# Seven block products for eight in the gate and up projections of a two-layer model

## The chip, the cores and the metric

One Trainium2 chip, one core of it. The metric is the device time of one execution in microseconds (us); the kernel before took 3628.52 us, the median of three runs (3627.12 to 3630.19). TensorE is called PE here, VectorE DVE, ScalarE ACT, GpSimd POOL, and SP is the engine that issues the DMAs.

## The reference, cut to what matters

A model of 512 tokens of width 1024 in float32: two layers of one kind, then two of another. Each of the latter is a feed-forward, a hybrid mixer and a second feed-forward, so the block below runs four times, with 1024 x 2816 gate and up weights and 2816 x 1024 down weights:

```python
def rmsnorm(x, w):
    xf = x.astype(jnp.float32)
    y = xf * lax.rsqrt(jnp.mean(xf * xf, axis=-1, keepdims=True) + EPS)
    return (y * w.astype(jnp.float32)).astype(x.dtype)

def swiglu(h, w_gate, w_up, w_down):
    return (jax.nn.silu(h @ w_gate) * (h @ w_up)) @ w_down
...
        x = x + 0.5 * swiglu(rmsnorm(x, norm_ffn1[layer]), ffn1_gate[layer], ffn1_up[layer],
                             ffn1_down[layer])
```

## The kernel before, in words

Activations lie feature-major: tile `X` is 128 partitions x 8 chunks x 512 tokens. Float32 products are made of three matmuls in a rounded format: every operand is split into a high part (ACT copies it into the rounded type) and a low part (DVE subtracts the high part from the original), and `mm3` adds high x high, high x low and low x high into one PSUM bank. So a product of a 1024-long contraction into 128 features is 8 x 3 matmuls, each with a 128x128 weight block loaded and 512 tokens streamed.

Weights come in one stream, `wall`: chunks of 128 x 512 floats, that is four 128x128 blocks, in the order in which they are used. `wfill` issues the DMA of a chunk on SP (256 KB), splits it on ACT and DVE, and runs `LOOK` = 3 chunks ahead; `w` hands out the blocks. High and low parts have four buffers each (`p_hi`, `p_lo`), raw chunks four.

`ffn` calls `rms_begin`, which splits X times the gain into `XH` and `XL` and makes `rb`, the reciprocal root of each token, on 128 partitions; since `rb` depends on the token alone it is multiplied into the products' results. Then J = 22 pairs follow: for each block of 128 hidden features a gate and an up product through `fm_seq` (the first three products interleaved over k, the others one by one). A gate result is multiplied by `rb` on DVE (L602) and goes through Silu on ACT (L603); an up result is multiplied by `rb` (L606) and by the gate (L607), and the pair is split at once into `HH` and `HL`, tiles of 22 chunks. The down products, m = 0 to 7, contract over the 22 chunks of `HH` and `HL`; each is added with weight 0.5 into `X[:, m]` (L612). In the very last feed-forward the eighth down product runs in two halves of 256 tokens.

The order of the instructions on an engine isn't that of the code: the framework sets it when the program is built, and an instruction can pass one that stands ahead of it in the code but isn't ready yet. Only what stands in `pin` keeps its place. A buffer of a pool is given to its next tile when the last use of the one before is over.

Of the kernel before, what the change touches and what calls it, by code (L numbers as in the profile page):

```python
# [7 lines left out]
F32 = mybir.dt.float32  # L8
F32R = mybir.dt.float32r
I32 = mybir.dt.int32  # L10
AF = mybir.ActivationFunctionType
OP = mybir.AluOpType
# [3 lines left out]
T = 512  # L16
D = 1024
KD = 8
DFF1 = 4096
DFF2 = 2816  # L20
CH = 512
NCH = 1104
NCOL = 332
NROW = 168
LOOK = 3
# [37 lines left out]
class Parts:  # L63


    def __init__(self, parts):
        self.parts = parts

    def __getitem__(self, i):
        return self.parts[i[1]]  # L70


class K:
    def __init__(self, tc, ap, inp):
        self.tc, self.nc, self.ap, self.inp = tc, tc.nc, ap, inp
        self.es = ExitStack()
        self.wall = np.zeros((NCH, 128, CH), np.float32)
        self.cols_a = np.zeros((128, NCOL), np.float32)
        self.rows_a = np.zeros((1, NROW), np.float32)
        self.ncol = 0  # L80
        self.nrow = 0
        self.wpos = 0
        self.wemit = 0
        self.look = LOOK
        self.wt = {}

    def pool(self, name, bufs, **k):
# [2 lines left out]

    def wfill(self, upto, pin=lambda i: i):
        nc = self.nc
        while self.wemit < min(upto, NCH):
            c = self.wemit
            raw = self.p_raw.tile([128, CH], F32, name="wraw")
            nc.sync.dma_start(out=raw, in_=self.ap['wall'][c])
            hi = self.p_hi.tile([128, CH], F32R, name="whi")
            pin(nc.scalar.activation(hi, raw, AF.Copy))  # L98
            lo = self.p_lo.tile([128, CH], F32R, name="wlo")
            pin(nc.vector.tensor_tensor(out=lo, in0=raw, in1=hi.bitcast(F32), op=OP.subtract))  # L100
            self.wt[c] = (hi, lo)
# [366 lines left out]
    def first_layer(self, i):  # L468
# [3 lines left out]
        with ExitStack() as es:  # L472
# [35 lines left out]
            for half in range(2):  # L508
                hh = []
                for name, n in HT[i]:  # L510
                    t = pool.tile([128, n, T], F32R, name=name)
                    hh += [t[:, k] for k in range(n)]
                HH, HL = Parts(hh[:16]), Parts(hh[16:32])
                o = half * 2048
                for m, ps in enumerate(self.fm_seq(XH, XL, [w1[:, o + m * 128:o + (m + 1) * 128] for m in range(16)])):
# [69 lines left out]


    def ffn(self, i, n):
        nc, inp = self.nc, self.inp
        with ExitStack() as es:
            pool = es.enter_context(self.tc.tile_pool(name="ffn%d%d" % (i, n), bufs=1, reuse_waits="tile"))  # L590
            XH, XL, y, rb = self.rms_begin(self.cols(inp['norm_ffn%d_2' % n][i]), pool if n == 2 else None)
            wg, wu, wd = [inp['ffn%d_%s_2' % (n, z)][i] for z in ('gate', 'up', 'down')]
            J = DFF2 // 128
            HH = pool.tile([128, J, T], F32R, name="HH")
            HL = pool.tile([128, J, T], F32R, name="HL")
            ws = []
            for j in range(J):
                ws += [wg[:, j * 128:(j + 1) * 128], wu[:, j * 128:(j + 1) * 128]]
            for j, ps in enumerate(self.fm_seq(XH, XL, ws)):
                if j % 2 == 0:  # L600
                    g1 = self.p_wk.tile([128, T], F32, name="t0")
                    nc.vector.tensor_tensor(out=g1, in0=ps, in1=rb, op=OP.mult)  # L602
                    nc.scalar.activation(g1, g1, AF.Silu)  # L603
                    continue
                u1 = self.p_wk.tile([128, T], F32, name="t1")
                nc.vector.tensor_tensor(out=u1, in0=ps, in1=rb, op=OP.mult)  # L606
                nc.vector.tensor_tensor(out=u1, in0=u1, in1=g1, op=OP.mult)  # L607
                self.split(HH[:, j // 2], HL[:, j // 2], u1)
            last = i == 1 and n == 2
            for m in range(7 if last else 8):  # L610
                ps = self.fm(HH, HL, wd[:, m * 128:(m + 1) * 128])
                nc.vector.scalar_tensor_tensor(out=self.X[:, m], in0=ps, scalar=0.5, in1=self.X[:, m], op0=OP.mult, op1=OP.add)  # L612
                if last:
                    self.sum_sq(m)
            if last:
                ws = [self.w(wd[k * 128:(k + 1) * 128, 896:]) for k in range(J)]
                self.out = self.p_x.tile([128, 8, T], F32, name="XH")
                for half in range(2):
                    s = slice(half * 256, half * 256 + 256)
                    ps = self.dps()  # L620
                    for k, (wh, wl) in enumerate(ws):
                        self.mm3(ps[:, :256], wh, wl, HH[:, k, s], HL[:, k, s], k == 0, k == J - 1)
                    self.final(half, s, ps[:, :256])
        return self.stop("ffn%d_%d" % (n, i))
# [1281 lines left out]
```

## Time and profile before

| | us |
|---|---|
| median of three runs | 3628.52 |
| the profiled execution's own time | 3626.38 |
| its span, first to last instruction | 3624.6 |
| PE busy | 3537.3 (98%) |
| DVE busy | 1980.6 (55%) |
| ACT busy | 1534.8 (42%) |
| POOL busy | 395.6 (11%) |

The shares are of the span and average over unlike stages. Matmuls overlap: a busy time of 389 ns for one says nothing of the step from one to the next, which is read from a timeline. The granted clock of PE was 0.995 of its full speed over the span.

### The profile page before, as it was taken

The page shows a single profiled execution, that of the slowest core. Times are in us where ns is not written, and L with a number is a line of the kernel's source. Part 1 is how long each engine was busy: PE and PEld are TensorE (multiplying, and loading weights), DVE is VectorE, ACT ScalarE, POOL GpSimd, SP SyncE. Part 2 cuts the span into 40 slices and gives each one's busy share as a digit, 9 for nine tenths or more (in the row PEclk, how much of TensorE's full clock was granted, in tenths as well). Part 3 has the DMA queues.
Part 4 walks back from the last instruction along what each step waited for, and adds up shares of the span by engine and source line. Part 5 has one row for each costly group of instructions (what it writes and reads, how often), then busy time and mean ns, then how long its engine had stood idle before and what let it go on. Part 6 is the DMA issues. An engine that isn't in the chain of part 4 may idle for free.

```text
span 3624.6 us, 46983 instructions
## 1 busy us (share of the span) xinstructions
PE 3537.3 (98%) x17270; PEld 2892.1 (80%) x17270; DVE 1980.6 (55%) x3841; ACT 1534.8 (42%) x2827; POOL 395.6 (11%) x402
## 2 busy tenths in 40 slices
PE   9999999999999999999999999999999999999999
PEld 7766888876678887888887888888888888888887
DVE  4686534467764346544368655543454378665443
ACT  4554524256643334433365533333333366443332
POOL 0003000203030003000012410000000012410000
PEclk9999999999999999999999999999999999999999
DMA  4112333332023332333332113333333332013332
GB/s 155 53 39 73 93 98 97 90 95 62 18 83 98 96 97 81 96 96 98 97 104 69 36 39 94 96 99 97 94 98 97 96 106 70 19 50 97 99 96 88
DMA packets 165976, 304.37 MB, mean 84 GB/s; under 512 B 19824, under 2 KB 20976, under 8 KB 165360
## 3 DMA queue, kind: packets, MB, share of 16 engines
q1 hardware_dynamic: 165744, 301.36, 28.6%
q8 instruction: 135, 2.21, 0.2%
q14 instruction: 97, 0.79, 0.1%
HBM read 299.19 MB, written 2.10 MB: 83 GB/s over the span
## 4 chain that ended last, share of the span: by engine, by line
PE 80%; DVE 6%; ACT 3%; issue 2%; POOL 1%; DVEq 0%; POOLq 0%; ACTq 0%
PE pd L246 24%; PE pd L245 24%; PE pd L247 24%; PE pt L264 1%; DVE wlo L100 1%; PE pd L1515 1%; PE ps L1503 1%; PE po L1747 0%; PE pd L1700 0%; ACT whi L98 0%; PE pd L1224 0%; DVE rep L1192 0%; PE ps L1239 0%; PE ps L1178 0%; PE ps L1240 0%
## 5 line engine op out<-in xcount | busy, mean ns | idle before, releaser
L100 DVE TENSOR_TENSOR wlo<-wraw,whi 128x512 fp32r<-128x512 f32 x1104 | 793.6, 720 | 1041.9 <-ACT whi L98 999.7
L98 ACT ACTIVATE whi<-wraw 128x512 fp32r<-128x512 f32 x1104 | 695.6, 631 | 1487.8 <-PE pd L246 1254.3
L245 PE MATMUL pd<-XH,whi 128*128 128x512 f32 x2752 | 1080.0, 394 | 22.2 <-DVE t L235 5.4
L246 PE MATMUL pd<-XL,whi 128*128 128x512 f32 x2752 | 1080.1, 392 | 12.1 <-DVE XL L411 9.5
L247 PE MATMUL pd<-XH,wlo 128*128 128x512 f32 x2752 | 1080.2, 393 | 0.0
L245 PEld LDWEIGHTS pd<-XH,whi 128*128 128x128 f32 x2752 | 518.6, 189 | 138.0 <-DVE t L235 6.3
L246 PEld LDWEIGHTS pd<-XL,whi 128*128 128x128 f32 x2752 | 520.0, 189 | 125.4 <-DVE XL L411 11.2
L247 PEld LDWEIGHTS pd<-XH,wlo 128*128 128x128 f32 x2752 | 519.6, 189 | 110.6 <-issue 2.6
L245 PE MATMUL pd<-HH,whi 128*128 128x512 f32 (+1 forms) x726 | 278.1, 383 | 0.0
L247 PE MATMUL pd<-HH,wlo 128*128 128x512 f32 (+1 forms) x726 | 277.7, 383 | 0.0
L246 PE MATMUL pd<-HL,whi 128*128 128x512 f32 (+1 forms) x726 | 277.6, 383 | 0.0
L454 POOL TENSOR_TENSOR acc<-acc,t 128x512 f32<-128x512 f32 x36 | 47.3, 1315 | 1162.3 <-ACT t L453 1151.4
L245 PEld LDWEIGHTS pd<-HH,whi 128*128 128x128 f32 x726 | 136.4, 188 | 26.9
L247 PEld LDWEIGHTS pd<-HH,wlo 128*128 128x128 f32 x726 | 136.4, 188 | 26.6
L246 PEld LDWEIGHTS pd<-HL,whi 128*128 128x128 f32 x726 | 136.4, 188 | 26.6
L606 DVE TENSOR_TENSOR t<-pd,rb 128x512 f32<-128x512 f32 x88 | 60.8, 691 | 86.7 <-PE pd L247 86.7
L602 DVE TENSOR_TENSOR t<-pd,rb 128x512 f32<-128x512 f32 x88 | 60.8, 691 | 82.7 <-PE pd L247 82.7
L245 PE MATMUL pd<-CQHL,whi 128*128 128x512 f32 x224 | 88.8, 397 | 0.0
L247 PE MATMUL pd<-CQHL,wlo 128*128 128x512 f32 x224 | 88.0, 393 | 0.0
L260 ACT ACTIVATE HH<-t 128x512 fp32r<-128x512 f32 x88 | 55.7, 633 | 50.6 <-DVE t L607 50.6
L344 POOL COPY acc<-X 128x512 f32<-128x512 f32 x4 | 3.1, 777 | 676.5 <-DVE X L342 527.9
L261 DVE TENSOR_TENSOR HL<-t,HH 128x512 fp32r<-128x512 f32 x88 | 60.9, 692 | 21.0 <-ACT HH L260 14.9
(809 smaller groups left out, 4945.0 us busy)
## 6 DMA issues: line engine op xcount, KB each, us to landing
wraw<-in_wall_dram SPq DMA_DIRECT2D x1104, 256.0 KB, 2.6
X<-in_xT_dram SPq DMA_DIRECT2D x8, 256.0 KB, 5.7
cw<-in_cw_dram SPq DMA_DIRECT2D x2, 1024.0 KB, 6.3
X<-in_xT_dram SPq DMA_DIRECT2D x1, 2048.0 KB, 8.2
out_dram<-XH SPq DMA_DIRECT2D x8, 256.0 KB, 2.7
t<-in_pT_dram SPq DMA_DIRECT2D x4, 256.0 KB, 2.8
LV<-in_cst_dram SPq DMA_DIRECT2D x2, 512.0 KB, 4.0
g_dT<-in_rgw_dram SPq DMA_DIRECT2D x2, 256.0 KB, 3.8
```

What stands on the lines that cost most here:

```text
L98: pin(nc.scalar.activation(hi, raw, AF.Copy))
L100: pin(nc.vector.tensor_tensor(out=lo, in0=raw, in1=hi.bitcast(F32), op=OP.subtract))
L245: t.matmul(ps, ah, bh, start=first, stop=False)
L246: t.matmul(ps, ah, bl, start=False, stop=False)
L247: t.matmul(ps, al, bh, start=False, stop=last)
L260: self.nc.scalar.activation(hi, src, AF.Copy)
L261: self.nc.vector.tensor_tensor(out=lo, in0=src, in1=hi.bitcast(F32), op=OP.subtract)
L264: self.nc.tensor.transpose(out, src, self.ID[:kp, :kp])
L454: (nc.vector if c == 7 else nc.gpsimd).tensor_tensor(out=acc, in0=acc, in1=sq, op=OP.add)
L602: nc.vector.tensor_tensor(out=g1, in0=ps, in1=rb, op=OP.mult)
L606: nc.vector.tensor_tensor(out=u1, in0=ps, in1=rb, op=OP.mult)
L1503: nc.tensor.matmul(pz[:, h], B[:, h], Xt[c][:, h], start=True, stop=True)
```

## The change: block products of Strassen's kind, and a result kept whole

Of the 22 pairs of a feed-forward the pairs 5 to 20 go through a new class, `Strassen`. It takes gate and up together as a matrix of two block rows (128 gate features, 128 up features) and two block columns (inputs 0 to 511 and 512 to 1023), and the tokens as two halves of 256. The 2 x 2 block product is then made from seven block products in the place of eight, with sums of weight blocks (s1 to s4, made on the chip for each pair) and sums of activation blocks (t0 to t3, made once a feed-forward), in Winograd's form: results of products are added up in PSUM over several of them, and partly on DVE and ACT.

- A `product` is 4 row blocks x 3 matmuls of 256 columns, 12 matmuls. `cycle(j)` issues seven: four of pair j into banks A, D and B with the weights a11, a12, s1 and s2, the fifth with s4, and between them two of pair j - 1 (s3 and a22) into its bank A.
- `load` fetches the four raw chunks of the next pair; `pa` splits a12 and a11, `sums` makes two sums, `ps` a third one and splits two of them; `ring` splits a block into the buffers of the weight stream.
- `c12` finishes the gate of the pair before, `c22` and `c21` the up part and the product into `H`.
- The activations must be normalised ahead, since sums of tokens' halves mix tokens with unlike `rb`: `prepare` makes X times gain times `rb` in `H[:, 14:22]`, the four sums and their splits `TH` and `TL`, during the five plain pairs. `renew` then overwrites `XH` and `XL` with the normalised ones.
- The pair's result stays in `H`, in whole float32, and is split into `HH` and `HL` only around the down products; these parts lie in the memory of tiles that are no longer needed. The first three down products run interleaved over k, the others one by one, and in the first feed-forward of a layer the last one begins with the low parts 16 to 21.
- The last pair, 21, is a plain one on the normalised activations, without `rb`.

```diff
...
@@ -67,7 +67,176 @@
         self.parts = parts
     def __getitem__(self, i):
-        return self.parts[i[1]]
+        p = self.parts[i[1]]
+        return p if len(i) == 2 else p[:, i[2]]
+class Strassen:
+    def __init__(self, k, pool, wg, wu, XH, XL, TH, TL, H):
+        self.k, self.nc, self.pool, self.wg, self.wu, self.H = k, k.nc, pool, wg, wu, H
+        self.XH, self.XL, self.TH, self.TL = XH, XL, TH, TL
+        self.R, self.u, self.prev = {}, {}, None
+        for name, n in self.PLACES:
+            pool.tile([128, n, T], F32, name=name)
+    PLACES = [("R0", 4), ("R1", 4), ("ST", 4), ("AH", 2), ("AL", 2), ("SH", 2), ("SL", 2), ("HX", 2)]
...
+    def prepare(self, X, gain, rb):
+        nc, H = self.nc, self.H
...
+        for c in range(8):
+            nc.vector.scalar_tensor_tensor(out=XN[:, c], in0=X[:, c], scalar=gain[:, c:c + 1], in1=rb, op0=OP.mult, op1=OP.mult)
+            if c % 2:
+                yield
+        b = lambda r, t: XN[:, 4 * r:4 * r + 4, 256 * t:256 * t + 256]
+        t = [H[:, 6 + 2 * q:8 + 2 * q].rearrange("p a (h t) -> p (a h) t", h=2) for q in range(4)]
+        nc.vector.tensor_tensor(out=t[0], in0=b(0, 0), in1=b(0, 1), op=OP.subtract)
+        yield
+        nc.vector.scalar_tensor_tensor(out=t[1], in0=t[0], scalar=-1.0, in1=b(1, 1), op0=OP.mult, op1=OP.subtract)
+        yield
+        nc.vector.tensor_tensor(out=t[2], in0=b(1, 1), in1=b(0, 1), op=OP.subtract)
+        yield
+        nc.vector.tensor_tensor(out=t[3], in0=b(0, 0), in1=b(1, 0), op=OP.subtract)
+        yield
+        nc.vector.tensor_tensor(out=t[3], in0=t[3], in1=t[2], op=OP.add)
+        yield
+        for q in range(4):
+            nc.scalar.activation(self.TH[:, q], t[q], AF.Copy)
+            yield
+            nc.vector.tensor_tensor(out=self.TL[:, q], in0=t[q], in1=self.TH[:, q].bitcast(F32), op=OP.subtract)
+            yield
+    def renew(self):
+        for c in range(8):
+            self.k.split(self.XH[:, c], self.XL[:, c], self.XN[:, c])
+    def load(self, j, c):
+        nc, k = self.nc, self.k
+        R = self.R[j] = self.pool.tile([128, 4, T], F32, name="R%d" % (j % 2))
+        s = slice(j * 128, (j + 1) * 128)
+        for q, (w, o) in enumerate(((self.wg, 4), (self.wg, 0), (self.wu, 4), (self.wu, 0))):
...
+        for q in (0, 1, 3, 2):
+            nc.sync.dma_start(out=R[:, q], in_=k.ap['wall'][c + q])
...
+    def ring(self, j, what, src):
+        hi, lo = self.k.p_hi.tile([128, CH], F32R, name="whi"), self.k.p_lo.tile([128, CH], F32R, name="wlo")
+        self.k.split(hi, lo, src)
+        self.u[j, what] = hi, lo
+    def pa(self, j):
+        hi, lo = self.parts("A", self.R[j][:, 0:2])
+        self.u[j, "a12"], self.u[j, "a11"] = [(hi[:, q], lo[:, q]) for q in range(2)]
+    def sums(self, j):
+        nc, R = self.nc, self.R[j]
+        S = self.S = self.pool.tile([128, 4, T], F32, name="ST")
+        nc.vector.tensor_tensor(out=S[:, 0:2], in0=R[:, 1:3], in1=R[:, 3:4].to_broadcast([128, 2, T]), op=OP.add)
+    def ps(self, j):
+        S = self.S
+        self.nc.vector.tensor_tensor(out=S[:, 2], in0=S[:, 1], in1=self.R[j][:, 1], op=OP.add)
+        hi, lo = self.parts("S", S[:, 1:3])
+        self.u[j, "s1"], self.u[j, "s2"] = [(hi[:, q], lo[:, q]) for q in range(2)]
+    def product(self, ps, w, x, first):
+        wh, wl = w
+        for r in range(4):
+            s = slice(r * 128, r * 128 + 128)
+            mm = lambda a, b, start, stop: self.nc.tensor.matmul(ps, a, b, start=start, stop=stop, skip_group_check=not first)
+            mm(wh[:, s], x(0, r), first and r == 0, False)
+            mm(wh[:, s], x(1, r), False, False)
+            mm(wl[:, s], x(0, r), False, r == 3)
+    def x(self, r0, t):
+        return lambda z, r: (self.XH, self.XL)[z][:, r0 + r, 256 * t:256 * t + 256]
+    def t(self, q):
+        return lambda z, r: (self.TH, self.TL)[z][:, q, r]
+    def cycle(self, j, more, c):
+        nc, k, u = self.nc, self.k, self.u
+        A, D, B = [k.bank(z)[:, :256] for z in "dst"]
+        p = self.prev
+        if p:
+            self.c12(p)
+            self.ring(j - 1, "a22", self.R[j - 1][:, 2])
+            self.ps(j)
+        self.product(A, u.pop((j, "a11")), self.x(0, 0), True)
+        g = k.p_wk.tile([128, T], F32, name="t0")
+        nc.scalar.activation(g[:, :256], A, AF.Copy)
+        if more:
+            self.load(j + 1, c)
+        if p:
+            self.product(p['A'], u.pop((j - 1, "s3")), self.t(2), False)
+            self.c22(p)
+        nc.vector.tensor_tensor(out=self.S[:, 3], in0=self.S[:, 2], in1=self.R[j][:, 0], op=OP.add)
+        self.ring(j, "s4", self.S[:, 3])
+        self.product(D, u.pop((j, "a12")), self.x(4, 0), True)
+        nc.vector.tensor_tensor(out=g[:, :256], in0=D, in1=g[:, :256], op=OP.add)
+        if p:
+            self.product(p['A'], u.pop((j - 1, "a22")), self.t(3), False)
+            self.c21(p)
+        if more:
+            self.pa(j + 1)
+        self.product(B, u.pop((j, "s1")), self.t(0), True)
+        v = k.p_wk.tile([128, T], F32, name="t1")
+        snap = self.pool.tile([128, 256], F32, name="HX")
+        nc.scalar.activation(snap, B, AF.Copy)
+        self.ring(j, "s3", self.S[:, 0])
+        self.product(A, u.pop((j, "s2")), self.t(1), False)
+        nc.scalar.activation(g[:, 256:], A, AF.Copy)
+        if more:
+            self.sums(j + 1)
+        self.product(B, u.pop((j, "s4")), self.x(4, 1), False)
+        self.prev = dict(j=j, A=A, B=B, g=g, v=v, snap=snap)
+    def c12(self, p):
+        self.nc.vector.tensor_tensor(out=p['g'][:, 256:], in0=p['B'], in1=p['g'][:, 256:], op=OP.add)
+        self.nc.scalar.activation(p['g'], p['g'], AF.Silu)
+    def c22(self, p):
+        self.nc.vector.scalar_tensor_tensor(out=p['v'][:, 256:], in0=p['A'], scalar=-1.0, in1=p['snap'], op0=OP.mult, op1=OP.subtract)
+    def c21(self, p):
+        self.nc.scalar.activation(p['v'][:, :256], p['A'], AF.Copy, scale=-1.0)
+        self.nc.vector.tensor_tensor(out=self.H[:, p['j']], in0=p['v'], in1=p['g'], op=OP.mult)
+    def tail(self, j):
+        p = self.prev
+        self.ring(j, "a22", self.R[j][:, 2])
+        self.c12(p)
+        self.product(p['A'], self.u.pop((j, "s3")), self.t(2), False)
+        self.c22(p)
+        self.product(p['A'], self.u.pop((j, "a22")), self.t(3), False)
+        self.c21(p)
 class K:
...
@@ -90,7 +260,7 @@
     def wfill(self, upto, pin=lambda i: i):
         nc = self.nc
-        while self.wemit < min(upto, NCH):
+        while self.wemit < min(upto, self.wlim):
             c = self.wemit
             raw = self.p_raw.tile([128, CH], F32, name="wraw")
             nc.sync.dma_start(out=raw, in_=self.ap['wall'][c])
@@ -585,36 +755,112 @@
     def ffn(self, i, n):
         nc, inp = self.nc, self.inp
+        J, S0, S1 = DFF2 // 128, 5, 21
         with ExitStack() as es:
             pool = es.enter_context(self.tc.tile_pool(name="ffn%d%d" % (i, n), bufs=1, reuse_waits="tile"))
-            XH, XL, y, rb = self.rms_begin(self.cols(inp['norm_ffn%d_2' % n][i]), pool if n == 2 else None)
+            gain = self.cols(inp['norm_ffn%d_2' % n][i])
+            XH, XL, y, rb = self.rms_begin(gain, pool if n == 2 else None)
             wg, wu, wd = [inp['ffn%d_%s_2' % (n, z)][i] for z in ('gate', 'up', 'down')]
-            J = DFF2 // 128
...
+            sl = lambda j: slice(j * 128, (j + 1) * 128)
+            cp, names = (pool, ("CH", "CL")) if n == 1 else (self.p_x, ("XH", "XL"))
+            TH, TL = [cp.tile([128, 8, T], F32R, name=z).rearrange("p (a r) (h t) -> p a (r h) t", a=4, h=2) for z in names]
+            H = pool.tile([128, J, T], F32, name="H")
+            st = Strassen(self, pool, wg, wu, XH, XL, TH, TL, H)
+            self.wpos += -self.wpos % CH
+            c0 = self.wpos // CH
+            self.wlim = c0 + 4 * S0
+            def plain(js, scale):
+                ws = []
+                for j in js:
+                    ws += [wg[:, sl(j)], wu[:, sl(j)]]
+                for q, ps in enumerate(self.fm_seq(XH, XL, ws, first=3 if scale else 1)):
+                    if q % 2 == 0:
+                        g1 = self.p_wk.tile([128, T], F32, name="t0")
+                        if scale:
+                            nc.vector.tensor_tensor(out=g1, in0=ps, in1=rb, op=OP.mult)
+                        nc.scalar.activation(g1, g1 if scale else ps, AF.Silu)
+                    else:
+                        u1 = ps
+                        if scale:
+                            u1 = self.p_wk.tile([128, T], F32, name="t1")
+                            nc.vector.tensor_tensor(out=u1, in0=ps, in1=rb, op=OP.mult)
+                        nc.vector.tensor_tensor(out=H[:, js[q // 2]], in0=u1, in1=g1, op=OP.mult)
+                    yield q
+            xp = st.prepare(self.X, gain, rb)
+            for q in plain(range(S0), True):
+                if q >= 1:
+                    for _ in range(4):
+                        next(xp, None)
+                if q == 6:
+                    st.load(S0, c0 + 4 * S0)
+                if q == 2 * S0 - 2:
+                    for _ in xp:
+                        pass
+                    st.pa(S0)
+                    st.sums(S0)
+                    st.ps(S0)
+            st.renew()
+            for j in range(S0, S1):
+                st.cycle(j, j + 1 < S1, c0 + 4 * (j + 1))
+            self.wemit = c0 + 4 * S1
+            self.wpos = self.wemit * CH
+            self.wlim = NCH
+            self.wfill(self.wemit + 2)
+            st.tail(S1 - 1)
+            hh = st.overlay()
+            done, ll = [], []
...
+            HH, HL = Parts(hh), Parts(ll)
+            def split(upto):
+                while len(done) < min(upto, J):
+                    k = len(done)
+                    nc.scalar.activation(HH[:, k], H[:, k], AF.Copy)
+                    nc.vector.tensor_tensor(out=HL[:, k], in0=H[:, k], in1=HH[:, k].bitcast(F32), op=OP.subtract)
+                    done.append(k)
+            for q in plain(range(S1, J), False):
+                split(3 * q + 3)
+            if n == 1:
+                low(self.p_x, "XL", 6)
+            else:
+                low(pool, "XH", 8)
+                low(pool, "XL", 8)
             last = i == 1 and n == 2
-            for m in range(7 if last else 8):
-                ps = self.fm(HH, HL, wd[:, m * 128:(m + 1) * 128])
+            def add(m, ps):
                 nc.vector.scalar_tensor_tensor(out=self.X[:, m], in0=ps, scalar=0.5, in1=self.X[:, m], op0=OP.mult, op1=OP.add)
                 if last:
                     self.sum_sq(m)
+            pss = [self.dps() for _ in range(3)]
+            for k in range(J):
+                split(k + 4)
+                for m, ps in enumerate(pss):
+                    wh, wl = self.w(wd[k * 128:(k + 1) * 128, sl(m)])
+                    self.mm3(ps, wh, wl, HH[:, k], HL[:, k], k == 0, k == J - 1)
+            for m, ps in enumerate(pss):
+                add(m, ps)
+            for m in range(3, 7 if last else 8):
+                add(m, self.fms(HH, HL, [wd[:, sl(m)]], list(range(16, J)) + list(range(16)) if n == 1 and m == 7 else None)[0])
             if last:
                 ws = [self.w(wd[k * 128:(k + 1) * 128, 896:]) for k in range(J)]
-                self.out = self.p_x.tile([128, 8, T], F32, name="XH")
+                self.out = H[:, 0:8]
                 for half in range(2):
                     s = slice(half * 256, half * 256 + 256)
                     ps = self.dps()
```

## Rows read from the trace of the kernel before

**Rows 1.** The page, part 1: engine, busy us, share of the span, instructions.

```profile
PE 3537.3 (98%) x17270; PEld 2892.1 (80%) x17270; DVE 1980.6 (55%) x3841; ACT 1534.8 (42%) x2827; POOL 395.6 (11%) x402
```

**Rows 2.** The page, part 4: the chain's share by line.

```profile
PE 80%; DVE 6%; ACT 3%; issue 2%; POOL 1%; DVEq 0%; POOLq 0%; ACTq 0%
PE pd L246 24%; PE pd L245 24%; PE pd L247 24%; PE pt L264 1%; DVE wlo L100 1%; PE pd L1515 1%; PE ps L1503 1%; PE po L1747 0%; PE pd L1700 0%; ACT whi L98 0%; PE pd L1224 0%; DVE rep L1192 0%; PE ps L1239 0%; PE ps L1178 0%; PE ps L1240 0%
```

**Rows 3.** Busy time by stretch: gate/up pairs, and the pairs before them.

```profile
core 0: us, PE busy (x) PEld busy (x) DVE busy (x) ACT busy (x) POOL busy (x), PEclk, DMA share, GB/s
1513.31:1687.39 174.08, 174.08 (x770) 144.19 (x769) 83.02 (x129) 60.43 (x96) 0.00 (x0) 1.00 0.33 97
1478.60:1522.40 43.80, 43.80 (x195) 36.28 (x194) 21.56 (x33) 16.89 (x27) 0.00 (x0) 1.00 0.31 92
```

**Rows 4.** DVE's timeline around the evacuation of two up products, sixteen pairs apart.

```profile
1512.10 0.69 DVE L606 TENSOR_TENSOR t<-pd,rb 128x512 f32<-128x512 f32 x1 [1.54 <-PE pd L247]
1512.71 0.68 DVE L100 TENSOR_TENSOR wlo<-wraw,whi 128x512 fp32r<-128x512 f32 x1
1513.31 0.69 DVE L607 TENSOR_TENSOR t<-t,t 128x512 f32<-128x512 f32 x1
...
1687.39 0.69 DVE L607 TENSOR_TENSOR t<-t,t 128x512 f32<-128x512 f32 x1
```

**Rows 5.** PE's timeline, last down product: first and last of 45 matmuls of 256.

```profile
3595.47 0.28 PE L245 MATMUL pd<-HH,whi 128*128 128x256 f32 x1
...
3600.74 0.28 PE L247 MATMUL pd<-HH,wlo 128*128 128x256 f32 x1
```

**Rows 6.** Groups by line and shape, end of the kernel: 256 elements.

```profile
L661 DVE SCALAR_TENSOR_TENSOR X<-pd,X 128x256 f32<-128x256 f32 x1 | 0.4, 425 | 1.2 <-PE pd L247 1.2
L663 ACT ACTIVATE t<-X 128x256 f32<-128x256 f32 x1 | 0.4, 418 | 2.4 <-DVE X L661 2.4
```

**Rows 7.** Groups of instructions by line, in the sixteen pairs.

```profile
L100 DVE TENSOR_TENSOR wlo<-wraw,whi 128x512 fp32r<-128x512 f32 x65 | 44.7, 687 | 30.6 <-ACT whi L98 30.5
L98 ACT ACTIVATE whi<-wraw 128x512 fp32r<-128x512 f32 x64 | 40.5, 633 | 86.0 <-PE pd L246 83.7 <-PE pd L247 2.4
```

**Rows 8.** Timeline of all engines: last matmul of a bank, and its reader.

```profile
3609.09 0.28 PE L247 MATMUL pd<-HH,wlo 128*128 128x256 f32 x1
...
3609.41 0.42 DVE L661 SCALAR_TENSOR_TENSOR X<-pd,X 128x256 f32<-128x256 f32 x1 [1.18 <-PE pd L247]
```

**Rows 9.** The page, part 6: DMA issues, KB each, median us to landing.

```profile
wraw<-in_wall_dram SPq DMA_DIRECT2D x1104, 256.0 KB, 2.6
...
cw<-in_cw_dram SPq DMA_DIRECT2D x2, 1024.0 KB, 6.3
```

**Rows 10.** ACT's timeline: `rb` is made.

```profile
1478.07 0.60 ACT L200 ACTIVATE rb<-pt 128x512 f32<-128x512 f32 x1 [2.11 <-PE pt L192]
```

**Rows 11.** Busy time by stretch: hybrid layer, and a stretch at low clock.

```profile
1836.00:2185.00 349.00, 332.00 (x2062) 283.06 (x2061) 241.40 (x515) 183.58 (x378) 84.91 (x88) 1.00 0.20 57
1417.20:1424.00 6.80, 5.60 (x13) 4.45 (x14) 6.76 (x11) 3.36 (x5) 0.60 (x1) 0.50 0.15 39
```

**Rows 12.** PE's timeline in that stretch: the wait at its start.

```profile
1418.40 0.80 PE L246 MATMUL pd<-XL,whi 128*128 128x512 f32 x1 [2.37 <-DVE XL L411]
```

**Rows 13.** PE's timeline: 256 columns, a new weight chunk.

```profile
3604.24 0.28 PE L247 MATMUL pd<-HH,wlo 128*128 128x256 f32 x1
3604.41 0.38 PE L245 MATMUL pd<-HH,whi 128*128 128x256 f32 x1
3604.63 0.28 PE L246 MATMUL pd<-HL,whi 128*128 128x256 f32 x1
```

**Rows 14.** PE's timeline: a bank's last matmul, the next bank's first.

```profile
1833.19 0.28 PE L246 MATMUL ps<-wlo,XH 128*128 128x264 f32 x1
1833.31 0.28 PE L247 MATMUL ps<-whi,XL 128*128 128x264 f32 x1
1833.43 0.28 PE L245 MATMUL pd<-whi,XH 128*128 128x264 f32 x1
```

More of the change, by code (lines that the diff above doesn't have):

```diff
@@ L21 @@
 CH = 512
-NCH = 1104
+NCH = 1112
 NCOL = 332
@@ L69, in __getitem__, with overlay, parts @@
     def __getitem__(self, i):
-        return self.parts[i[1]]
+        p = self.parts[i[1]]
[8 more added lines that the diff above has]
+    PLACES = [("R0", 4), ("R1", 4), ("ST", 4), ("AH", 2), ("AL", 2), ("SH", 2), ("SL", 2), ("HX", 2)]
+    def overlay(self):
+        hh = []
+        for name, n in self.PLACES:
+            t = self.pool.tile([128, n, T], F32R, name=name)
+            hh += [t[:, k] for k in range(n)]
+        return hh
+    def prepare(self, X, gain, rb):
+        nc, H = self.nc, self.H
+        XN = self.XN = H[:, 14:22]
+        for c in range(8):
[27 more added lines that the diff above has]
+        for q, (w, o) in enumerate(((self.wg, 4), (self.wg, 0), (self.wu, 4), (self.wu, 0))):
+            k.wall[c + q] = w[o * 128:o * 128 + 512, s].reshape(4, 128, 128).transpose(1, 0, 2).reshape(128, CH)
+        for q in (0, 1, 3, 2):
+            nc.sync.dma_start(out=R[:, q], in_=k.ap['wall'][c + q])
+    def parts(self, name, src):
+        hi, lo = [self.pool.tile([128, 2, T], F32R, name=name + z) for z in "HL"]
+        self.nc.scalar.activation(hi, src, AF.Copy)
+        self.nc.vector.tensor_tensor(out=lo, in0=src, in1=hi.bitcast(F32), op=OP.subtract)
+        return hi, lo
+    def ring(self, j, what, src):
[78 more added lines that the diff above has]
+        self.c21(p)
@@ L594, in ffn @@
[L594 to L608, printed above, removed]
+            sl = lambda j: slice(j * 128, (j + 1) * 128)
@@ new lines, in ffn, with low @@
+            self.wemit = c0 + 4 * S1
+            self.wpos = self.wemit * CH
+            self.wlim = NCH
+            self.wfill(self.wemit + 2)
+            st.tail(S1 - 1)
+            hh = st.overlay()
+            done, ll = [], []
+            def low(p, name, n):
+                t = p.tile([128, n, T], F32R, name=name)
+                ll.extend(t[:, k] for k in range(n))
+            if n == 1:
+                low(pool, "CH", 8)
+                low(pool, "CL", 8)
+            else:
+                low(self.p_x, "XH", 6)
@@ new lines, in ffn @@
+            HH, HL = Parts(hh), Parts(ll)
[7 more added lines that the diff above has]
+                split(3 * q + 3)
+            if n == 1:
+                low(self.p_x, "XL", 6)
+            else:
+                low(pool, "XH", 8)
+                low(pool, "XL", 8)
```

## The prediction, made before the change was run

> **What bounds the kernel now.** The first part of the page comes first: the reader is to see that TensorE (PE) is busy for 98% of the span, VectorE (DVE) for 55% and ScalarE (ACT) for 42% [rows 1]. The chain that ended last says the same: 80% of it is PE, and three lines, those of `mm3`, hold 72% [rows 2]. Then the stage of the change: over sixteen gate/up pairs of the first feed-forward, PE is busy for all of 174.08 us, at full clock, and DVE for 83 of them [rows 3]. The same evacuation recurs there every 10.88 us (174.08 / 16) [rows 4]. A pair is 48 matmuls of 512 columns, so one starts every 226.7 ns and nothing is waited for. What counts here is therefore how long PE's own queue is; the other engines count only if they come late.
>
> **PE, the gain.** Seven block products replace eight, each on half the tokens. One product is 4 row blocks x 3 matmuls = 12 of 256 columns, a pair 7 x 12 = 84 of them in place of 48 of 512. In columns that is 7/8, but the fixed part of a matmul is paid 84 times. The trace has the very form, in the last down product: 45 of them, the first at 3595.47 and the last at 3600.74 us, 44 steps of 119.8 ns [rows 5]. 84 x 0.1198 = 10.06 us against 10.88: 0.82 us less for a pair, 13.1 us for the 16 pairs of one feed-forward, 52.3 us for four. The five plain pairs ahead, the one behind and all down products keep their matmuls; the down products only change their order.
>
> **DVE and ACT within a cycle.** A cycle of `Strassen` brings DVE six operations of 128x512 (the low parts of a22, s4 and s3, the third and fourth sum, the product into `H`), three of 128x1024 (the low parts of `pa` and `ps`, `sums`) and three of 256 out of PSUM. Three DVE operations of 512 in a row start 0.605 us apart, though each shows 0.69 [rows 4]; one of 256 shows 0.425 [rows 6], 0.26 less, so I take 0.34 for its step. None of 1024 is in these rows; by the same slope it steps by 1.13, at most it is two of 512, 1.38. Sum: 6 x 0.605 + 3 x 1.13 + 3 x 0.34 = 8.0 us; at the most, 6 x 0.69 + 3 x 1.38 + 3 x 0.425 = 9.6. Both are under 10.06, so DVE isn't the bound, but it goes from 48% to 80 or 95% busy. ACT has four of 512 at 0.633 [rows 7], two of 1024 (at most 1.27) and four of 256 at 0.418 [rows 6]: at most 6.7 us.
>
> Does each arrive in time? Products start 1.44 us apart: P1 at 0, P2 1.44, P3 2.88, P4 4.31, P5 5.75, P6 7.19, P7 8.63. A reader of PSUM starts 0.32 us after the start of the last matmul, 0.2 after the next product's start [rows 8]. The closest hand-over is `c22`: it reads the bank that P2 has just filled and P4 adds to, so it is ready at 3.08 and must be through by 4.31, and one long operation may stand before it (1.13 + 0.34 leads to 4.55 in the worst case, 0.24 late). The copy of B behind P5 has the same 1.44 us, on the emptier ACT. The other deadlines have some 2 us: `ps` is wanted at 5.75, s4 at 8.63. The weights of the next pair are four DMAs of 256 KB, issued once the a22 block has been read, at about 1.9; a lone one lands in 2.6 us and one of 1024 KB in 6.3 [rows 9], so the first two are there by some 5.5, the last by 8.2; `pa`, which PE wants at 10.06, needs the first two and 2.1 us of ACT and DVE: 7.6 to 8.1. The SP queue has nothing else to issue there. I take 0.05 us of stall a cycle (bounds 0 and 0.24), 0.8 us for 16.
>
> **Entry.** During the five plain pairs `prepare`, `pa`, `sums` and `ps` add to DVE 8 normalised chunks (4.8 us), 9 operations of 1024 (10.2), and 4.0 for the first pair: 19 us. From 1478.6, when `rb` is there [rows 10], to 1522.4, where the ninth product ends, the same stretch now has 21.6 us of DVE [rows 3], of which 2.8 are low parts of `HL` that go away. With seven of the eight `renew` splits (4.2) that makes 42 of 43.8 us: full, without room. `renew` overwrites XH and XL, chunk by chunk as the last plain product leaves them. If it ran in the order of the code, eight low parts would stand behind the last two evacuations: XL[7] at 0.2 + 10 x 0.605 = 6.2 us, wanted at 1.44 + 9 x 0.12 = 2.5, 3.7 us late. But the instructions are put in order by readiness, not by the code: at 1512.7 a weight split stands between two evacuations that follow one another in the code [rows 4]. Then most low parts come first, and I take 1.5 us (bounds 0 and 3.7 and, with DVE behind, 6).
>
> **Exit.** In `tail` the last two products add to one bank with `c22` between them and nothing else of the cycle: 0.2 + 0.43 + some 0.1 = 0.7 us, which the next plain product can fill if it is put there. I take 0.6 (0 to 1.5). The down products get their split of H from ACT and DVE during them: 22 x 0.69 us of DVE that was spent in the gate/up stage before; a column block of three products takes 9 x 0.227 = 2.04 us of PE and needs one H split and 0.75 weight split, 1.2 us of DVE: hidden. The eight more chunks of the weight stream are padding. Transitions to the next layer stand as before, since the low parts that lie in XH and XL are read first in the last product.
>
> **Sum.** A feed-forward: -13.1 + 0.8 + 1.5 + 0.6 = -10.2 us, four: -40.7. The profiled execution took 3626.38 us (span 3624.6), 2.1 less than the median of the runs, 3628.52. So 3585.7 on the former, 3588 on the latter.
>
> **A rule against it.** The granted clock stayed at its 2.4 GHz level through the hybrid layer, 349 us with PE waiting for 17 of them [rows 11]. It fell to 1.2 GHz in a stretch in which PE idled 2.4 us for a low part, and thirteen matmuls of 512 then took 5.6 us, 0.43 each [rows 11, 12]. The Trainium skill (TensorE: Matmul & The Clock Gate, "A second HAM failure mode: psum-queue depth-cycling") tells of a kernel that cycled through PSUM banks and idled briefly between groups until the clock oscillated. The cycle here changes bank with each product, every 1.44 us, so by that rule its short waits would suffice. As a mechanism of this kernel: if a fifth of 64 x 10.06 = 644 us ran at the lower level, 129 us of work would take 1.9 times as long, +113, and the time would be 3700. The hybrid layer's rows speak against it; 2%.
>
> **Rivals.** (1) *The entry is in code order, or DVE is late there.* 4 to 6 us four times is 16 to 24 in place of 6: 3598 to 3606. With a DVE so full that `c22` comes 0.2 us late in every cycle (10 more than I took) it is up to 3616. For it: the 42 of 43.8 us. Against: the order by readiness. 22%.
> (2) *DVE sets the cycle.* If operations start no closer than their shown length and wait for the weights besides, 9.6 us + 1 of waiting is 10.6: 64 x 0.28 = 18 us of gain less 10 of transitions, 3620; at 10.8 nothing is left. Against: the steps of 0.605. 6%.
> (3) *Slower: the weight load at the start of each product is exposed.* Where a 256-column matmul waited for its chunk, two steps were 0.17 and 0.22 us instead of 0.12, 0.15 us lost [rows 13]: PE had nothing queued over which to load. A cycle has seven such places, and nothing of 512 columns beside them: 7 x 0.15 x 64 = 67 us, so 3628.5 - 52.3 + 67 + 8 = 3651. It decides from 0.117 us a product on (0.82 / 7). Against it: with products of 264 columns, whose weights were there, PE goes from one bank to the next, at a new chunk, in 0.12 us [rows 14]. The price is paid only where DVE or ACT are late. 6%.
>
> **How the numbers follow.** Forecast, 3576 to 3604: 64%. Rival 1: 22%, rival 2: 6%, rival 3: 6%, the clock: 2%. The least that can come is PE's own arithmetic, 3628.5 - 52.3 = 3576. The range, 3575 to 3614, holds the forecast and most of rival 1. A change of 0.2% (7 us) is about what can be told from none. Faster: 0.64 + 0.22 and a third of rival 2, 0.88; the same 0.04; slower 0.08.
>
> **What would show it.** PE: 2304 more matmuls (16 x 4 x 36); in `product` 0.12 us from one to the next and a pair every 10.1 us; `c22` done before P4. Right at the entry: idle PE of 1 to 2 us before the first cycle's third product, four times. Wrong: a cycle over 10.4, PE waiting for `whi`/`wlo` or `c22` in each, a clock below full within the stage, or an entry of 4 us and more.

## The result and the profile after

The changed kernel takes 3585.45 us (median of 4 runs, 3581.69 to 3586.11) against 3628.96 for the kernel before on the same chip (4 runs, 3627.12 to 3630.19): the ratio is 0.9878, its 95% interval 0.9861 to 0.9895, 43.5 us less. The profiled execution took 3584.97 us with a span of 3583.2, 41.4 under the span before. Line numbers below are those of the changed kernel: 172 is the matmul of `product`, 415 to 417 are `mm3`, 268 and 270 the halves of a weight chunk (`whi`, `wlo`), 431 is the low part of a split, 142 and 143 are the two parts of `pa` and `ps`, 159 is `sums`, and 103 to 121 are `prepare`.

Part 1 of the page after answers to [rows 1]:

```profile
PE 3487.8 (97%) x19574; PEld 2958.2 (83%) x19574; DVE 2270.2 (63%) x4256; ACT 1734.7 (48%) x3198; POOL 397.0 (11%) x402
```

PE has 2304 matmuls more, 16 x 4 x 36, and still is 49.5 us less busy. DVE was given 290 us of work. The chain that ended last, after, answers to [rows 2]:

```profile
PE 86%; DVE 7%; ACT 3%; issue 2%; POOL 1%; DMA 1%; DVEq 0%; ACTq 0%; POOLq 0%
PE pd L415 19%; PE pd L416 19%; PE pd L417 19%; PE pd L172 10%; PE pt L172 5%; PE ps L172 3%; PE pt L434 2%; DVE wlo L270 1%; PE pd L1761 1%; PE ps L1749 1%; PE ps L1238 1%; PE po L1214 1%; ACT whi L268 1%; PE po L1993 0%; PE pd L1946 0%
```

PE still sets the end: `mm3` now holds 57% of the chain, the block products 18%. Busy time by stretch, after, answers to [rows 3]; the first stretch lies within the block products of the first feed-forward, the second over the plain pairs ahead of them, from the making of `rb` on:

```profile
core 0: us, PE busy (x) PEld busy (x) DVE busy (x) ACT busy (x) POOL busy (x), PEclk, DMA share, GB/s
1527.50:1685.00 157.50, 157.50 (x1313) 157.42 (x1312) 127.71 (x188) 95.88 (x168) 0.00 (x0) 1.00 0.30 96
1484.70:1527.40 42.70, 40.56 (x178) 33.06 (x177) 35.55 (x49) 20.91 (x32) 0.00 (x0) 1.00 0.23 74
```

In the first, PE never stops: 157.50 us over 1313 matmuls is 0.120 us each, at full clock, and DVE is busy for 81% where it was 48%. In the second, PE is 2.1 us short of full. Before, a stretch of that kind was full.

DVE's timeline over one cycle, and the same operation eleven cycles later, answers to [rows 4]:

```profile
1559.81 0.68 DVE L200 TENSOR_TENSOR ST<-ST,R 128x512 f32<-128x512 f32 x1
...
1564.69 1.23 DVE L143 TENSOR_TENSOR SL<-ST,SH 128x1024 fp32r<-128x1024 f32 x1 [1.80 <-ACT SH L142]
1565.83 0.42 DVE L222 TENSOR_TENSOR t<-pt,t 128x256 f32<-128x256 f32 x1
1566.16 0.68 DVE L431 TENSOR_TENSOR wlo<-ST,whi 128x512 fp32r<-128x512 f32 x1
...
1568.36 0.68 DVE L164 TENSOR_TENSOR ST<-ST,R 128x512 f32<-128x512 f32 x1
1568.96 0.68 DVE L431 TENSOR_TENSOR wlo<-R,whi 128x512 fp32r<-128x512 f32 x1
...
1569.89 0.68 DVE L200 TENSOR_TENSOR ST<-ST,R 128x512 f32<-128x512 f32 x1
...
1670.69 0.68 DVE L200 TENSOR_TENSOR ST<-ST,R 128x512 f32<-128x512 f32 x1
```

Line 200 comes back after 10.08 us, and ten cycles on after 100.8 more. Next to each other, an operation of 1024 steps by 1.14, one of 256 by 0.33, one of 512 by 0.60.

PE's timeline where one product ends and the next begins in another bank, answering to [rows 14]:

```profile
1528.76 0.28 PE L172 MATMUL pd<-XH,AL 128*128 128x256 f32 x1
1528.88 0.28 PE L172 MATMUL ps<-XH,AH 128*128 128x256 f32 x1
1529.00 0.28 PE L172 MATMUL ps<-XL,AH 128*128 128x256 f32 x1
```

0.12 us again: nothing is exposed at the start of a product.

### The profile page after: what moved, and what is told of

Read it like the earlier page. It is cut to its first block, busy times and chain, and to the rows that moved or that the text cites. A ratio compares the mean times of both kernels' runs of the same rounds, so it can differ in the third digit from the quotient of the medians.

```text
span 3583.2 us, 52604 instructions
## 1 busy us (share of the span) xinstructions
PE 3487.8 (97%) x19574; PEld 2958.2 (83%) x19574; DVE 2270.2 (63%) x4256; ACT 1734.7 (48%) x3198; POOL 397.0 (11%) x402
## 4 chain that ended last, share of the span: by engine, by line
PE 86%; DVE 7%; ACT 3%; issue 2%; POOL 1%; DMA 1%; DVEq 0%; ACTq 0%; POOLq 0%
PE pd L415 19%; PE pd L416 19%; PE pd L417 19%; PE pd L172 10%; PE pt L172 5%; PE ps L172 3%; PE pt L434 2%; DVE wlo L270 1%; PE pd L1761 1%; PE ps L1749 1%; PE ps L1238 1%; PE po L1214 1%; ACT whi L268 1%; PE po L1993 0%; PE pd L1946 0%
## 5 line engine op out<-in xcount | busy, mean ns | idle before, releaser
L270 DVE TENSOR_TENSOR wlo<-wraw,whi 128x512 fp32r<-128x512 f32 x851 | 619.2, 730 | 748.8 <-ACT whi L268 735.4
L268 ACT ACTIVATE whi<-wraw 128x512 fp32r<-128x512 f32 x851 | 535.5, 630 | 1036.0 <-PE pd L416 896.3
L416 PE MATMUL pd<-XL,whi 128*128 128x512 f32 (+1 forms) x1960 | 770.2, 393 | 11.8 <-DVE XL L581 9.5
L415 PE MATMUL pd<-XH,whi 128*128 128x512 f32 x1728 | 682.4, 398 | 23.5 <-DVE t L405 5.4
L417 PE MATMUL pd<-XH,wlo 128*128 128x512 f32 x1728 | 681.0, 394 | 5.0 <-DVE wlo L270 5.0
L416 PEld LDWEIGHTS pd<-XL,whi 128*128 128x128 f32 x1960 | 371.1, 189 | 93.3 <-DVE XL L581 11.7
L415 PEld LDWEIGHTS pd<-XH,whi 128*128 128x128 f32 x1728 | 326.3, 189 | 99.6 <-DVE t L405 6.3
L417 PEld LDWEIGHTS pd<-XH,wlo 128*128 128x128 f32 x1728 | 327.2, 189 | 76.9 <-DVE wlo L270 6.2
L415 PE MATMUL pd<-R,whi 128*128 128x512 f32 (+1 forms) x264 | 101.5, 384 | 0.0
L417 PE MATMUL pd<-R,wlo 128*128 128x512 f32 (+1 forms) x264 | 101.0, 383 | 0.0
```

The costliest lines, as they stand in the source:

```text
L415: t.matmul(ps, ah, bh, start=first, stop=False)
L416: t.matmul(ps, ah, bl, start=False, stop=False)
L417: t.matmul(ps, al, bh, start=False, stop=last)
```

## Where the rest of the gain went

PE's arithmetic alone was worth 52.3 us; 43.5 came. Of the 8.8 us that lack little is in the cycles: 10.08 us for the 10.06 of the forecast makes 1.1 in 64 pairs. PE's waits, after, over the whole span (engine and line, what was waited for, us in total, times, longest) give the only row that the new stage adds:

```profile
PE pd L417 <- DVE wlo L270: 5.0, 3, 2.0
```

It lies in the plain pairs ahead of the block products, 2.05, 1.50, 0 and 1.50 us in the four feed-forwards. PE's timeline at the first of them:

```profile
1495.75 0.39 PE L416 MATMUL pd<-XL,whi 128*128 128x512 f32 x1
1495.98 0.28 PE L172 MATMUL pt<-CH,SH 128*128 128x256 f32 x1
1498.30 0.50 PE L417 MATMUL pd<-XH,wlo 128*128 128x512 f32 x1 [2.05 <-DVE wlo L270]
```

The matmul due at 1496.10 starts at 1498.30 and the next is 0.11 us late once more, 2.3 in all. (A single block-product matmul has been put ahead of the wait.) DVE's timeline shows what stood ahead of `wlo`:

```profile
1493.03 1.21 DVE L108 TENSOR_TENSOR H<-H 128x1024 f32<-128x1024 f32 x1
1494.16 1.22 DVE L112 TENSOR_TENSOR H<-H 128x1024 f32<-128x1024 f32 x1
1495.30 1.21 DVE L110 SCALAR_TENSOR_TENSOR H<-H 128x1024 f32<-128x1024 f32 x1
1496.43 1.22 DVE L114 TENSOR_TENSOR H<-H 128x1024 f32<-128x1024 f32 x1
1497.57 1.28 DVE L270 TENSOR_TENSOR wlo<-wraw,whi 128x512 fp32r<-128x512 f32 x2
```

Four sums of `prepare`, 4.5 us in one piece, of which PE needs nothing before the block products but for the one matmul above, stand in DVE's queue ahead of two low parts that PE needs at 1496.1 (by ACT's timeline their high parts were done at 1490.3 and 1493.0). Elsewhere DVE had time. Its timeline around the making of `rb`, later now than in [rows 10]:

```profile
1476.52 1.22 DVE L143 TENSOR_TENSOR AL<-R,AH 128x1024 fp32r<-128x1024 f32 x1
...
1478.65 1.22 DVE L159 TENSOR_TENSOR ST<-R 128x1024 f32<-128x1024 f32 x1
...
1482.06 1.22 DVE L143 TENSOR_TENSOR SL<-ST,SH 128x1024 fp32r<-128x1024 f32 x1
...
1485.29 0.75 DVE L103 SCALAR_TENSOR_TENSOR H<-X,COL,rb 128x512 f32<-128x512 f32 x1 [1.18 <-ACT rb L370]
```

`pa`, `sums` and `ps` of the first block pair are done before `rb` is, and DVE then idles 1.18 us. That room was not free: this work stands between the small DVE operations that lead to `rb` (lines 440 to 449), and `rb` now comes 16.8 us after the first matmul of the feed-forward (1484.66 and 1467.85, by the timelines of ACT and PE); before, it came after 12.2 (1478.07 in [rows 10] and 1465.88). The splits of `renew` came early enough too, by DVE's timeline at the end of the plain pairs:

```profile
1523.55 0.69 DVE L431 TENSOR_TENSOR XL<-H,XH 128x512 fp32r<-128x512 f32 x1
...
1525.30 3.09 DVE L431 TENSOR_TENSOR XL<-H,XH 128x512 fp32r<-128x512 f32 x5
1528.31 0.68 DVE L791 TENSOR_TENSOR t<-pd,rb 128x512 f32<-128x512 f32 x1
```

Six low parts of the new XL ran before the evacuation of the last plain product (line 791), and PE went from the last plain matmul at 1527.22 to the first block product at 1527.45, 0.23 us later: no wait. The exit costs a little, by PE's timeline in `tail`:

```profile
1687.76 0.39 PE L417 MATMUL pd<-XH,wlo 128*128 128x512 f32 x1
1688.16 0.36 PE L172 MATMUL pd<-CH,whi 128*128 128x256 f32 x1
1688.35 0.28 PE L172 MATMUL pd<-CL,whi 128*128 128x256 f32 x1
```

Steps of 0.40 and 0.19 where 0.23 and 0.12 were due: 0.24 us, although three plain matmuls had been put between the last two products. Measured from the first matmul of a feed-forward to the first of the next stage, the four gained 9.6, 10.4, 12.3 and 10.4 us, 42.7 together; the third, which has no wait for `wlo`, comes nearest to the 13.1 of the arithmetic, and with the wait and its late restarts added back all four stand at 11.9 to 12.3. (The span gained less, 41.4: in this execution the first of them began 2.0 us later than before.)

## The experiments

My theory: all of the gain is PE's arithmetic, 0.82 us a pair; what lacks is the order of DVE's work at the entry, not its amount. The rivals: the gain, or part of it, comes from keeping H whole; the cycle hides a DVE bound or a late `c22`; the entry is full, so that fewer plain pairs or more block pairs cost more than they bring.

**e1_whole: H kept whole, no block products.** Pairs 0 to 20 are plain too.

```diff
-            xp = st.prepare(self.X, gain, rb)
-            for q in plain(range(S0), True):
...
-            st.tail(S1 - 1)
+            self.wlim = NCH
+            for q in plain(range(J - 1), True):
+                pass
-            for q in plain(range(S1, J), False):
+            for q in plain(range(J - 1, J), True):
```

> All 22 pairs plain, none by block products; H is still kept whole and split only around the down products, which keep their new order. Theory (the gain is PE's arithmetic, 64 pairs by 0.8 us): nothing of it is left, 3629 us, within 4 us of the kernel before. Rival (the gain comes from taking the split of H out of the gate/up stage): most of it stays, 3585 to 3605.

Measured: 3627.1 us, ratio 1.0001 (0.9992 to 1.0011). The whole H, its later split and the new order of the down products give and cost nothing; that rival falls.

**e2_half: eight block pairs instead of sixteen.**

```diff
-        J, S0, S1 = DFF2 // 128, 5, 21
+        J, S0, S1 = DFF2 // 128, 5, 13
...
-                split(3 * q + 3)
+                split(min(3 * q + 3, 6))
```

The second hunk lets the longer row of plain products behind the block products split no more than the six chunks of H that were split there before.

> Pairs 5 to 12 by block products, 8 in place of 16 in each feed-forward; entry and exit are the same. Theory: 32 pairs go back from 10.08 to 10.88 us, 3585.5 + 32 x 0.80 = 3611 us. Rival (what is won is won once a feed-forward, at its ends): 3585 to 3590.

Measured: 3609.7 us, 0.9952 (0.9938 to 0.9967). From no block pair to 8 it is 17.4 us, from 8 to 16 it is 24.3, and 8 pairs in four feed-forwards are worth 26.2 by the arithmetic. So the gain grows with the pairs and the loss, 8.8 us in both, is paid once per transition, 2.2 us a feed-forward, as far as intervals of some 5 us on each time can tell. The wait for `wlo` was there (2.06 us), and here the granted clock fell right behind it. Busy time by stretch, e2:

```profile
1497.80:1501.20 3.40, 3.40 (x9) 2.63 (x8) 3.40 (x6) 1.15 (x2) 0.00 (x0) 0.50 0.48 154
```

Nine matmuls of 512 in 3.4 us, their starts 0.43 apart as in the stretch of [rows 11], cost 1.6 us more than at full clock. In the change itself the same wait had no such sequel in the first feed-forward.

**e3_dve4 and e4_dve10: four, and ten, more DVE operations in each cycle**, of 256 elements, into a tile that nobody reads.

```diff
         if more:
             self.sums(j + 1)
+            S = self.S
+            DX = self.pool.tile([128, 256], F32, name="DX")
+            for _ in range(4):
+                nc.vector.tensor_tensor(out=DX, in0=S[:, 3, :256], in1=S[:, 3, 256:], op=OP.add)
```

> Four idle operations of 128x256 more on DVE in each cycle (61 of them), into a tile that nobody reads. Theory (DVE's operations step 0.34 us and 8.0 of 10.06 us are taken): 9.4 us, still under PE's cycle; PE doesn't wait more than 0.1 us a cycle, 3585 to 3592. Rival 2 of the prediction (they cost their shown length, 0.42, on top of 9.6): 11.3 us a cycle, 60 x 1.2 = 72 us more, 3657. Rival (the hand-over of c22 is at its limit): a long wait in each cycle, 0.3 us or more, 3603 and up.

Measured: 3586.61 us, 0.9889 (0.9872 to 0.9905). Busy time by stretch within the block products, e3:

```profile
1530.00:1685.00 155.00, 154.91 (x1290) 154.64 (x1290) 145.03 (x237) 95.12 (x168) 0.00 (x0) 1.00 0.31 99
```

DVE is busy for 94% and PE still starts a matmul every 0.120 us. With 1.3 us more on DVE next to nothing in the cycle is late (counted by 84 matmuls, one cycle of each feed-forward takes 10.3 or 10.4 us, the next 10.2, the others 10.08): the rivals of a DVE bound and a late `c22` fall.

> Ten such operations a cycle. Theory: 8.0 + 3.4 = 11.4 us of DVE, now the bound; the cycle is 11.4 to 11.6, 60 x 1.4 = 84 us more, 3665 to 3680, and the change would be a loss of 40 us. Rival 2 (shown lengths): 9.6 + 4.2 = 13.8 us, 60 x 3.7, 3807.

Measured: 3720.0 us, 1.0257 (1.0242 to 1.0273), some 40 above what I expected. Ten steps of 0.334 on 8.03 make 11.4 us; the 1094 matmuls below, 84 to a cycle, make 12.3 us a cycle on PE. Busy time by stretch, e4: the stage, and three neighbouring stretches in it.

```profile
1540.00:1700.00 160.00, 143.22 (x1094) 137.40 (x1093) 151.29 (x277) 72.16 (x126) 0.00 (x0) 0.97 0.26 85
1585.00:1588.20 3.20, 1.74 (x13) 1.32 (x12) 3.17 (x7) 2.62 (x4) 0.00 (x0) 1.00 0.00 0
1588.20:1591.60 3.40, 3.40 (x19) 3.40 (x18) 3.26 (x9) 0.38 (x1) 0.00 (x0) 0.50 0.23 52
1591.60:1595.00 3.40, 3.13 (x26) 2.92 (x25) 1.90 (x6) 1.53 (x3) 0.00 (x0) 1.00 0.73 261
```

PE's waits in that stage, e4:

```profile
PE pd L172 <- DVE t L230: 7.0, 9, 1.1
PE pt L172 <- ACT SH L142: 4.9, 6, 1.0
PE pt L172 <- DVE SL L143: 3.5, 5, 0.7
```

At 0.12 us each, the 1094 matmuls need 131.3 of the 160 us. PE idles 16.8, 15.4 of it in the 20 waits of these three rows; the other 11.9 are slower matmuls, those at the lower clock and those around each wait. `c22` (line 230 there), the tightest place of the cycle by the prediction, and the parts of `ps` are what comes late. Counted by 84 matmuls, most cycles of the later half take 11.55 and 13.07 us in turn, 12.3 in the mean, and 1.5 more where the clock falls within one; twelve falls in the four stages are some 18 of the 134.6 us that e4 took above the change. That waits in the queue make 12.3 of 11.4 is what the rows suggest; why every other cycle is the longer one, I did not settle.

**e5_rate2: `prepare` drawn two steps per plain product instead of four**, so that fewer of its operations stand in DVE's queue at once.

```diff
                 if q >= 1:
-                    for _ in range(4):
+                    for _ in range(2):
                         next(xp, None)
```

> prepare is drawn two steps after each plain product instead of four, so the sums t0 to t3 stand behind the weight split that PE waited for (2.0, 1.5 and 1.5 us in three feed-forwards). Theory (what is missing of the arithmetic is this order on DVE, not DVE's load): these waits go, none comes at the first cycle, 6 us less, 3577 to 3581. Rival (DVE is full up to the first cycle): the wait only moves to the first cycles, 3584 to 3588.

Measured: 3578.24 us, 0.9863 (0.985 to 0.9877). The wait for `wlo` is gone. Busy time of the plain pairs, e5, and DVE's timeline there:

```profile
1484.70:1527.40 42.70, 42.62 (x201) 35.51 (x200) 38.52 (x55) 21.73 (x33) 0.00 (x0) 1.00 0.22 71
```

```profile
1495.41 1.22 DVE L110 SCALAR_TENSOR_TENSOR H<-H 128x1024 f32<-128x1024 f32 x1
1496.55 1.29 DVE L270 TENSOR_TENSOR wlo<-wraw,whi 128x512 fp32r<-128x512 f32 x2
1497.75 0.69 DVE L785 TENSOR_TENSOR t<-pd,rb 128x512 f32<-128x512 f32 x1
1498.35 1.22 DVE L112 TENSOR_TENSOR H<-H 128x1024 f32<-128x1024 f32 x1
```

DVE does more in the stretch than in the change (38.52 against 35.55 us) and PE is full: it was the order. 7.2 us of the missing 8.8 came back; the three waits with their late restarts sum to 5.9, and the intervals cover the difference.

**e6_s22, e7_rate2_s22: the last pair made a block pair too** (17 instead of 16), alone and with e5's edit. The places of the low parts of H are dealt anew, since no plain product stands behind the block products.

```diff
-        J, S0, S1 = DFF2 // 128, 5, 21
+        J, S0, S1 = DFF2 // 128, 5, 22
...
-            for q in plain(range(S1, J), False):
-                split(3 * q + 3)
...
```

> The last pair goes through the block products too, 17 pairs a feed-forward and no plain pair behind them; the low parts' places are dealt so that the first ones lie in tiles that are free by then. Theory (0.8 us a pair): 3.2 us less, 3581 to 3583. Rival (the plain pair is what hides the first splits of H): PE waits 1.3 us or more for the first split in each feed-forward, 3584 to 3590.

> Both edits. By the theories 9 us less than the change, 3575 to 3578; by the rivals 3584 or more.

Measured: e6 3580.75 us, 0.9871 (0.9858 to 0.9885), which its interval does not tell from the change; e7 3573.63, 0.985 (0.9837 to 0.9864), 1.4 us under the range that I expected. Against e5 in the same set of runs, e7 is 4.6 us faster and their runs don't overlap (3571.91 to 3574.2, 3576.81 to 3579.05); the arithmetic of one pair, four times, is 3.3. The plain pair behind the block products hid nothing that was needed.

**e8_rate2_s22_s4, e9_rate2_s22_s3: four, then three plain pairs ahead** (18 and 19 block pairs), on top of e7; in e9 the first block pair's weights are loaded at the third plain product.

```diff
-        J, S0, S1 = DFF2 // 128, 5, 22
+        J, S0, S1 = DFF2 // 128, 4, 22
```

> Both edits, and the block products begin one pair earlier: 18 pairs, and prepare has four plain pairs to go beside. PE's arithmetic alone: 3.2 us less than with both edits, 3572 to 3575. DVE's load: 42 us of work less the 5 of the fifth pair, in 33 us: 4 us late in each feed-forward, 3585 to 3592. I hold the second likelier.

Measured: 3572.38 us, 0.9849 (0.9835 to 0.9862): not the 3585 to 3592 that I held likelier, but no worse than e7, and not distinguishable from it. My count of the entry's DVE work was too high: what lay before `rb` already (above) is not in that stretch.

> As the run with 18 pairs, but 19 pairs and three plain pairs ahead of them (the first raw weights are fetched four products earlier for it). In the run with 18, DVE was busy for 33.3 of the 34.4 us between rb and the first block product. One pair less takes 10.9 us from that stretch and 4.5 us of DVE's work: 28.8 us of work in 23.5. Theory (DVE has become the bound there): PE waits 4 to 5 us in each feed-forward, 0.8 comes back by the pair, 3572.4 + 4 x 3.7 = 3587, range 3582 to 3592. Rival (the order moves enough of it ahead of rb or behind the first cycles): 3568 to 3571.

Measured: 3588.38 us, 0.989 (0.9874 to 0.9907), as expected. Busy time by stretch from `rb` on: e8, whose block products begin at 1511.85; e9 in the same way; then e9's plain pairs, which end at 1500.94, and the first block products behind them.

```profile
1482.40:1516.80 34.40, 34.30 (x171) 28.92 (x170) 33.28 (x47) 20.12 (x30) 0.00 (x0) 1.00 0.20 62
```

```profile
1482.40:1512.00 29.60, 26.44 (x127) 21.92 (x126) 28.27 (x38) 16.24 (x26) 0.00 (x0) 0.94 0.12 36
1482.40:1500.94 18.54, 18.46 (x82) 14.94 (x80) 17.93 (x24) 12.14 (x18) 0.00 (x0) 1.00 0.19 57
1500.94:1512.00 11.06, 7.97 (x47) 6.98 (x46) 10.34 (x15) 4.10 (x9) 0.00 (x0) 0.85 0.00 0
```

PE's waits, e9, from 1482.40 to 1512.00:

```profile
PE pd L172 <- DVE XL L431: 2.1, 2, 1.5
PE pt L172 <- ACT HX L212: 1.0, 1, 1.0
```

In e8, DVE is busy for 97% of the stretch and PE is full. In e9, PE is full as long as the plain pairs last, with DVE again busy for 97%; behind them it idles 3.1 of 11.1 us, 2.1 of them for the low parts of the new XL, with a fall of the clock besides (0.85). That is `renew` at the start of the first cycle, the place at which the prediction looked for the loss. So the entry's DVE work does become the bound, between four plain pairs and three, not at five. The best versions, e7 and e8, are 12 to 13 us under the change and some 55 under the kernel before.

## Why the prediction was right, point by point

**The arithmetic of PE** held nearly to the row: 0.1198 us a matmul was taken from [rows 5], 0.120 was measured, and the steps across banks were the same as in [rows 14]. e2 gives it by itself: 8 pairs on or off are 24.3 us where 26.2 were due, with an interval of about 5 on each time (and the kernel before 1.9 us apart in the two sets of runs).

**DVE in the cycle**: 8.0 us was forecast; the steps measured (0.60, 1.14, 0.33) give 6 x 0.60 + 3 x 1.14 + 3 x 0.33 = 8.0. The stall of 0.05 us a cycle that I added was none, 0.8 us a feed-forward too much; e3 shows that 1.3 us more make 0.3 to 0.5 in a whole feed-forward. Weights: the page after gives 3.6 us for the landing of an R block, between the 2.6 and 6.3 of [rows 9].

**The entry** was right in size (1.5 us forecast; 2.3, 1.8, 0 and 1.8 measured) and wrong in its reason. I saw DVE as full, 42 of 43.8 us, and looked for the loss in `renew` at the start of the first cycle. There it was nothing: by readiness, six of the low parts went first. The loss stood 30 us earlier, where four sums that nobody waits for were queued ahead of a weight's low part. The same sum of operations in another order (e5) loses nothing. The step that failed is the count: 4.0 us for the first pair lay before `rb`, at the price of a later `rb`, so DVE was busy for 38.5 of 42.7 us in e5 and the stretch had room, as e8 showed. Only with three plain pairs (e9) does the loss come where I looked for it, and for the reason that I gave.

**The exit**: 0.24 us in the first feed-forward for the 0.6 that I took. With it the sum of a feed-forward, -10.2, stands beside 9.6, 10.4, 12.3 and 10.4 gained. Over the four, the entry was 6.0 in the forecast and 5.9 in the rows; the stall (3.2) was none and the exit (2.4) some 1.0, if all are like the first; against that the cycles gave 1.1 less, and some 1.6 us are in no row that I found. That the total came within 3 us owes something to these, which partly cancel, and to an entry of the right size at another place.

**The rivals.** The first (an entry of 4 to 6 us) did not come; its place was misread, as above. The second falls by e3. The third falls by the step from bank to bank. The clock: it stayed at 1.00 through the block products. The Trainium skill's rule (TensorE: Matmul & The Clock Gate, "A second HAM failure mode: psum-queue depth-cycling") speaks of micro-idles between groups of matmuls as banks are cycled through, and PE had none here, so by this trace the change of banks alone does nothing. In e4, where PE idled 0.7 to 1.1 us at several places of a cycle, the clock did fall, 12 times in the four stages, each time for about 3.4 us (four of these in last cycles, which had one wait of 2.9 us); there the rule and the trace agree. A price of 113 us (129 x 0.9 would be 116) was not reached: in e4's stretch of 160 us all slower matmuls together cost 11.9.

## What to carry to other kernels

Count a product's time as the number of matmuls times the step of that very shape in the trace, not as columns: here 84 x 0.1198 against 48 x 0.2267 left 0.82 us of a nominal eighth (1.36). When such an exchange moves work to an engine that was half idle, look at the order of its queue, not only at its sum: four long operations that nobody awaits, drawn too early, cost some 6 us at three places, and drawing them half as fast brought this back without removing one. Then move the border between the old and the new form until the helper engine is really full: a busy share of 97% was still free of loss, one pair further was not.

## What the runs showed of the hardware

- A queue over its budget cost more than its sum: 3.3 us added to an 8.0 us load on DVE gave a cycle of 12.3 us on PE, not 11.4 (e4), part of it the lower clock, while 1.3 added left 10.08 but for two cycles of a feed-forward (e3).
- One wait of 2.06 us was followed by 3.4 us at a granted clock of 0.50 in e2; the wait of 2.05 us at the same place in the change was not. Over the first block products of e9, with waits of up to 1.5 us, the mean was 0.85. So a wait of this size may cost some 1.6 us on top, and the profiled execution does not say in advance whether it will.
- Operations of DVE that follow each other start 0.08 to 0.09 us before the one ahead is shown to end, at each of the three sizes (0.60 for 0.68, 1.14 for 1.23, 0.33 for 0.42).
